# Token-mixing work of GpSimd on VectorE and ScalarE, S5 states reordered by ScalarE, modulation sums copied out by ScalarE

## The chip, the cores and the metric

One core of a Trainium2 chip runs the program. It has TensorE (PE in the profile, its weight loads PEld), VectorE (DVE), ScalarE (ACT), GpSimd (POOL) and SyncE (SP), which issues most of the transfers. The metric is the device time of one execution in microseconds, the median of several runs.

## The reference

Two layers work on 512 latent tokens and 256 context tokens of 1024 features, in float32. Of each layer:

```python
sh1, sc1, g1, sh2, sc2, g2 = ada_params(c, w_mod, b_mod)      # silu(c) @ w_mod + b_mod; the same for the context
mix = token_mixers(layer_norm(x) * (1 + sc1) + sh1, ...)
x = layer_norm(ALPHA * x + g1 * mix, ln1_g, ln1_b)
x = layer_norm(ALPHA * x + g2 * conv_ffn(layer_norm(x) * (1 + sc2) + sh2, ...), ln2_g, ln2_b)

def token_mixers(h):
    u, xl, g = split(h @ w_in)                # 512 columns each
    y  = s5_readout(s5_states of u, both directions) + d * u     # 32 groups of 16 channels, 64 complex states
    y  = gelu(y); y = y * sigmoid(y @ w_glu + b_glu)
    yl = (lru_forward + lru_backward)(conv4(xl)) * gelu(g)       # gated linear scans
    return concat(y, yl) @ w_out
```

`conv_ffn` is a gated up projection to 2 x 2816, a 3x3 depthwise convolution on the latent grid, gelu, and a down projection. The last layer gives latent tokens only.

## The kernel before, in words

Matrix products keep float32 accuracy by splitting each operand into a rounded high half and the low remainder, with three products per chunk (`mm3`, lines 165 to 172). `split` (158 to 163) makes the halves: the high one on ScalarE (or on the engine in `hi_eng`), the low one, a subtraction of 1024 columns for a weight, on the engine that is passed. `halves` (196 to 202) loads a weight and passes GpSimd for every weight of the program. `HIE = 'SG'` puts the high halves of the input projection's weights on ScalarE in layer 0 and on GpSimd (line 162) in layer 1.

A layer is one stretch of mixing, one of the output projection, one of the feed-forward part. Mixing goes over eight blocks `hb` of four S5 groups. `prep` builds a block's tables: two `outer` products (589 to 600, six operations of 512 columns each), in layer 0 one on GpSimd and one on VectorE, in layer 1 loaded from DRAM, then transposes and small products whose result goes through DRAM into `tm`. `enter` (693 to 712) makes the block's chunk inputs on PE, copies them out shifted by one chunk, in reverse order for the backward half of the partitions, and lets GpSimd spread the decay `r8` into `rt` (709). `leave` (714 to 744) turns the inputs by phase tables, scans them (727), turns them back, writes the states with six operations (735 to 738), the backward half in reverse order again, and PE makes the outputs from them. Between the blocks the list `FILL` puts projections (`u_part`, `x_part`, `g_part`) and LRU parts (`lru_part`, 771 to 814; line 813 sums the two directions on GpSimd). `glu` closes the S5 side, and lines 1023 and 1024 split the LRU side.

The phase tables (`s5_params`, 565 to 578) are products of coarse and fine phases; line 575 to 577 run once on GpSimd for the cosine half and once on VectorE for the sine half. Layer 1's are made during layer 0's feed-forward part.

`mods` (288 to 329) multiplies the condition with `w_mod` in 16 steps. Parts q = 1 and 2 run as filler beside the mixing. At the end VectorE adds a bias row of 256 KB to the PSUM sums (315), the gate is stored to DRAM (318), PE transposes the rest (323) and VectorE takes two of every 32 columns into `modc` (328).

The residual sum (826), the power of the normalization (352, 366) and the low halves of all other weights are GpSimd's in every stage. The order of each engine's instructions is made by a list scheduler from priorities and its own time model.

Of the kernel before, what the change touches and what calls it, by code (L numbers as in the profile page):

```python
# [21 lines left out]
DEPTH = 2  # L22
# [18 lines left out]
HIE = 'SG'  # L41
# [11 lines left out]
def body(ctx: ExitStack, tc: tile.TileContext, a, out):  # L53
# [87 lines left out]
    def small(shape):  # L141
        count[0] += 1
        n = int(np.prod(shape[1:]))
        return cp.tile(list(shape), F32, name=f"{where[0]}_st_{count[0]}", tag=f"st{n}", bufs={12: 4, 4: 8, 1: 6}[n])
# [11 lines left out]
    hi_eng = [None]  # L156
# [39 lines left out]
    def halves(src, hi, lo):  # L196

        raw = raws(hi.shape)
        with behind(hold[0]):
            weight_load[0] = load(raw, src)  # L200
        split(raw, hi, lo, G)
        return hi, lo
# [77 lines left out]
    def row_of(l, q, row_ring, load=load):  # L280
        where[0] = f"mod{l}{q}"
        row = row_ring([128, 2, 256])
        load(row, a["b_mod"][l, q])
        return row
# [3 lines left out]
    def mods(l, q, raw_ring, row_ring, bank, depth=2, bias_load=load, after=None):  # L288
# [3 lines left out]
        row = None if row_ring is raw_ring else row_of(l, q, row_ring, bias_load)  # L292
# [20 lines left out]
        if row is None:  # L313
            row = row_of(l, q, row_ring)
        V.tensor_add(row, ps, row)
        if q > 0:
            for t in range(4):
                load(gd[l][q - 1, :, 256 * t:256 * t + 256], row[32 * t:32 * t + 2, q - 1, :])
        tp = bank().rearrange("p (i r) -> p i r", i=4)
        hs = {0: (0, 1), 1: (1,), 2: (0,)}[q]  # L320
        for h in hs:
            for j in range(2):
                PE.transpose(tp[:, 2 * h + j, :], row[:, h, 128 * j:128 * j + 128], ident)
        for h in hs:
            base = {0: 8 * h, 1: 16, 2: 24}[q]
            add = 1.0 if q == 2 or (q == 0 and h == 1) else 0.0
            for j in range(2):
                V.tensor_scalar(modc[l][:, base + j:base + 8:2, :],
                                tp[:, 2 * h + j, :].rearrange("p (t w) -> p t w", w=32)[:, :, 0:2], add, None, op0=ADD)
# [112 lines left out]
    def s5_params(l, scratch, raw_slots, phase_slots, cs_slots, tmp_slot, load=load):  # L442
# [122 lines left out]
        for hb in range(8):  # L565
            yield
            step()
            gs = slice(4 * hb, 4 * hb + 4)
            cs = new(cs_slots[hb % 2], [128, 2, 4, 96])
            tt = new(tmp_slot, [128, 2, 4, 96])  # L570
            bh = lambda i: hi[:, i, gs].unsqueeze(3).to_broadcast([128, 4, 12, 8])
            bl = lambda i: lo[:, i, gs].unsqueeze(2).to_broadcast([128, 4, 12, 8])
            w = lambda x: x.rearrange("p g (a b) -> p g a b", b=8)
            for i, e, op in ((0, G, SUB), (1, V, ADD)):
                e.tensor_tensor(w(cs[:, i]), bh(0), bl(i), op=MUL)
                e.tensor_tensor(w(tt[:, i]), bh(1), bl(1 - i), op=MUL)
                e.tensor_tensor(cs[:, i], cs[:, i], tt[:, i], op=op)
            nc.sync.dma_start(csd[l, hb], cs.rearrange("p i g n -> p (i g n)"))
# [41 lines left out]
    class S5:  # L620
# [29 lines left out]
        def prep(self, hb):  # L650
# [6 lines left out]
            if l == 0:  # L657
                outer(fo, hb, 2, prm["cc"], False, G, self.tg)
                outer(ein, hb, 0, prm["bb"], True, V, self.tv)
            else:  # L660
                load(ein.rearrange("p i g j c -> p (i g j c)"), tabd[hb, 0])
                load(fo.rearrange("p i g j c -> p (i g j c)"), tabd[hb, 1])
# [30 lines left out]
        def enter(self, hb, et):  # L693
# [15 lines left out]
            G.tensor_scalar(rt, self.prm["r8"][:, gs].unsqueeze(2).to_broadcast([128, 4, 96]), 1.0, None, op0=MUL)  # L709
# [4 lines left out]
        def leave(self, hb, fo2, tm):  # L714
# [32 lines left out]
    class LRU:  # L747
# [23 lines left out]
        def __call__(self, m, xc, bank):  # L771
# [41 lines left out]
            G.tensor_tensor(hs[0][:, 0:keep], hs[0][:, 0:keep], hs[1][:, 0:keep], op=ADD)  # L813
# [38 lines left out]
    start = mods(0, 0, ring("m0", "m1", "v0", "v1", "a0", "a1", "a3", "r0", "r1"), ring("gs"), banks("p4"), 9, S.dma_start)  # L852
# [17 lines left out]
    for l in range(DEPTH):  # L870
# [4 lines left out]
        cols, coef = par[l]  # L875
        if l > 0:
# [8 lines left out]
        filler = itertools.chain(*(mods(l, q, md_r, md_r, md_b, after=first_w) for q in (1, 2)))  # L885
# [137 lines left out]
        for m in range(4):  # L1023
            split(ge[0][:, m, 0:ntok], ylru[m][0][:, 0:ntok], ylru[m][1][:, 0:ntok], G)
# [3 lines left out]
        where[0] = f"out{l}"  # L1028
        gt = new("v", [128, 2, D])
# [161 lines left out]
        nxt = iter(()) if last else mods(l + 1, 0, md_r, md_r, md_b)  # L1191

        def next_layer():

            par.append(columns(l + 1))
            yield
# [57 lines left out]
def lay_out(x):  # L1254
# [5 lines left out]
    y["b_mod"] = np.repeat(cut(x["b_mod"], 3, 2, 4, 256).transpose(0, 1, 3, 2, 4), 32, axis=2)  # L1260
# [41 lines left out]
```

## Time and profile before

| | us |
|---|---|
| median of 3 runs | 1757.7 (1757.34 to 1763.57) |
| the profiled execution | 1757.56 |
| its span | 1755.8 |
| busy in it: PE / DVE / ACT / POOL | 1562.5 / 1302.9 / 648.1 / 807.7 |
| layer 0: mixing | about 60 to 305 |
| layer 0: glu, output, feed-forward | 305 to about 1000 |
| from layer to layer | 1000 to 1060 |
| layer 1: mixing and glu | 1060 to 1300 |
| layer 1: output and feed-forward | 1300 to the end |

Busy is the time in which an engine has at least one instruction between its start and its end; an instruction that stands waiting for a resource after its start counts as busy. Idle time of an engine that is not the bottleneck costs nothing.

### The profile page before, as it was taken

What the parts mean: (1) busy time and instruction counts of PE and PEld (TensorE: products, weight loads), DVE (VectorE), ACT (ScalarE), POOL (GpSimd) and SP (SyncE); (2) the same over time, 40 slices, a digit from 0 to 9 for tenths busy, and PEclk for the clock granted to TensorE, in tenths of its full rate; (3) what the DMA queues carried; (4) which work ended last, traced back from release to release, by engine and by line L of the source; (5) the groups of instructions that cost most, each with busy time, mean ns of one, the idle gap of its engine ahead of it and who ended that gap; (6) DMA issues with size and microseconds to landing.
All of it is one profiled execution on the core that took longest, in us unless ns stands there. A gap on an engine that the chain in (4) does not pass through costs nothing. (4 is left out here: it accounts for less than half of the span.)

```text
span 1755.8 us, 22958 instructions
## 1 busy us (share of the span) xinstructions
PE 1562.5 (89%) x8824; PEld 1267.1 (72%) x8824; DVE 1302.9 (74%) x2104; ACT 648.1 (37%) x941; POOL 807.7 (46%) x496
## 2 busy tenths in 40 slices
PE   4768778898999999999999779989869899999996
PEld 1656655677888787887888658767547888888884
DVE  7999999478566995677689883889557476555587
ACT  2426445633633222222222136344661643323320
POOL 2567543548332244522325383533156454444474
PEclk8788898999899999999999898998879899999998
DMA  8335435742221212423334315665463333232231
GB/s 332 105 114 162 136 113 185 231 154 92 78 72 61 96 49 97 156 109 131 118 118 150 111 52 185 212 213 171 152 209 125 102 120 108 84 108 96 85 120 60
DMA packets 95359, 227.10 MB, mean 129 GB/s; under 512 B 28912, under 2 KB 39696, under 8 KB 95248
## 3 DMA queue, kind: packets, MB, share of 16 engines
q1 hardware_dynamic: 85456, 212.92, 36.3%
q10 hardware_dynamic: 9792, 12.71, 2.0%
q8 instruction: 69, 1.13, 0.3%
q14 instruction: 42, 0.34, 0.1%
HBM read 194.50 MB, written 31.10 MB: 128 GB/s over the span
## 5 line engine op out<-in xcount | busy, mean ns | idle before, releaser
L170 PE MATMUL banks<-ar,ar 128*128 128x512 f32 (+2 forms) x2152 | 777.6, 367 | 49.1 <-ACT ar L160 16.8
L171 PE MATMUL banks<-ar,ar 128*128 128x512 f32 (+2 forms) x2152 | 778.3, 363 | 17.3 <-DVE ar L396 7.8
L172 PE MATMUL banks<-ar,ar 128*128 128x512 f32 (+2 forms) x2152 | 770.9, 362 | 2.3 <-DVE ar L163 2.2
L163 POOL TENSOR_TENSOR ar<-ar,ar 128x1024 fp32r<-128x1024 f32 (+1 forms) x184 | 456.0, 2485 | 572.2 <-ACT ar L160 479.5
L170 PEld LDWEIGHTS banks<-ar,ar 128*128 128x128 f32 x2152 | 412.8, 193 | 134.0 <-ACT ar L160 20.8
L171 PEld LDWEIGHTS banks<-ar,ar 128*128 128x128 f32 x2152 | 415.7, 193 | 82.9 <-DVE ar L396 9.7
L172 PEld LDWEIGHTS banks<-ar,ar 128*128 128x128 f32 x2152 | 415.5, 193 | 65.7 <-DVE ar L163 4.2
L160 ACT ACTIVATE ar<-ar 128x1024 fp32r<-128x1024 f32 (+3 forms) x236 | 226.1, 976 | 496.7 <-PE banks L171 202.1
L1141 DVE SCALAR_TENSOR_TENSOR ar<-banks,cols,ar 128x441 f32<-128x441 f32 (+2 forms) x352 | 243.1, 691 | 41.8 <-ACT ar L1136 35.0
L1175 DVE TENSOR_TENSOR ar<-banks,ar 128x512 f32<-128x512 f32 x160 | 109.0, 685 | 117.4 <-PE banks L172 115.4
L163 DVE TENSOR_TENSOR ar<-ar,ar 128x512 fp32r<-128x512 f32 (+1 forms) x64 | 77.8, 1228 | 56.0 <-ACT ar L160 39.1
L826 POOL TENSOR_TENSOR ar<-ar 128x512 f32<-128x512 f32 x40 | 62.2, 1560 | 47.8 <-DVE ar L822 47.1
L1148 ACT ACTIVATE ar<-ar,cols 128x768 f32<-128x768 f32 (+1 forms) x44 | 36.6, 831 | 122.2 <-DVE ar L1141 71.4
L185 PE MATMUL banks<-ar,cond 128*32 128x256 f32 x192 | 64.8, 441 | 18.9 <-DMA ar<-in_w_mod_dram 18.9
L384 PE MATMUL banks<-ident,ar 128*128 128x128 f32 x176 | 36.5, 345 | 34.4 <-ACT ar L358 16.4
L188 PE MATMUL banks<-ar,cond 128*32 128x256 f32 x576 | 65.8, 441 | 0.0
L396 DVE TENSOR_TENSOR ar<-ar,ar 128x256 fp32r<-128x256 f32 (+1 forms) x64 | 41.4, 666 | 32.9 <-ACT ar L395 32.6
L783 PE MATMUL banks<-ar,ar 128*128 128x512 f32 (+1 forms) x128 | 54.7, 550 | 7.8 <-issue 6.9
L162 POOL TENSOR_SCALAR ar<-ar 128x1024 fp32r<-128x1024 f32 x12 | 35.5, 2958 | 49.2 <-PE banks L171 27.5
L384 PEld LDWEIGHTS banks<-ident,ar 128*128 128x128 f32 x176 | 26.2, 175 | 41.5 <-ACT ar L358 17.4
L1136 ACT ACTIVATE ar<-banks,cols 128x512 f32<-128x512 f32 x44 | 29.9, 679 | 69.7 <-PE banks L172 69.6
L185 PEld LDWEIGHTS banks<-ar,cond 128*32 128x32 f32 x192 | 15.8, 115 | 54.8 <-DMA ar<-in_w_mod_dram 32.4
(255 smaller groups left out, 1921.0 us busy)
## 6 DMA issues: line engine op xcount, KB each, us to landing
ar<-in_w_mod_dram SPq DMA_DIRECT2D x96, 512.0 KB
ar<-in_ffn_w_up_dram SPq DMA_DIRECT2D x88, 512.0 KB
ar<-in_ffn_w_down_dram SPq DMA_DIRECT2D x44, 512.0 KB
ar<-in_w_in_dram SPq DMA_DIRECT2D x24, 512.0 KB
tabd<-ar SPq DMA_DIRECT2D x16, 512.0 KB
ar<-tabd SPq DMA_DIRECT2D x16, 512.0 KB
csd<-ar SPq DMA_DIRECT2D x16, 384.0 KB
ar<-csd SPq DMA_DIRECT2D x16, 384.0 KB
```

The source lines that it names most:

```text
L160: S.activation(hi, src, AF.Copy)
L163: return lo_eng.tensor_tensor(lo, src, hi.bitcast(F32), op=SUB)
L170: PE.matmul(ps, wh, xh, start=first and k == 0, stop=False)
L171: PE.matmul(ps, wh, xl, start=False, stop=False)
L172: PE.matmul(ps, wl, xh, start=False, stop=last and k == nk - 1)
L185: ins = PE.matmul(*args, **kw)
L188: ins = PE.matmul(*args, **kw)
L384: PE.transpose(tp[:, o:o + 128], z[:, 128 * k:128 * k + 128], ident)
L783: PE.matmul(gp, w[:, d, i, :], xc[:, o:o + n], start=True, stop=True)
L826: G.tensor_tensor(xs_t[:, cs], xs_t[:, cs], tmp, op=ADD)
L1141: inst[0] = V.scalar_tensor_tensor(av[:, yo, xo], uv[:, yi, xi], tap(1 + dy, 1 + dx, ch), av[:, yo, xo], op0=MUL, op1=ADD)
L1175: V.tensor_tensor(acc, ps, acc, op=ADD)
```

## The change

- High halves of layer 1's input weights go from GpSimd to ScalarE (`HIE`), low halves of all weights loaded in the mixing (input projection and glu) from GpSimd to VectorE (`lo_eng`); from the output projection on they stay on GpSimd.
- GpSimd's `outer` product, its half of the phase tables, the sum of the LRU directions and the LRU side's low halves go to VectorE, the spread of `r8` to ScalarE.
- `leave` combines the turned states with two operations of full partitions on VectorE, and ScalarE copies them into `st` in three pieces (two in layer 1), reversed for the backward half.
- `mods`: ScalarE copies the sums out of PSUM, PE transposes them, ScalarE copies the used columns out, and VectorE adds the bias there, from a small table `modb`. A bias row is loaded for gates only, 128 KB, after the sums are there. The transposes use named places of PSUM.
- One of the four buffers for normalization statistics goes.

```diff
-HIE = 'SG'
+HIE = 'SS'
@@ halves
-        split(raw, hi, lo, G)
+        split(raw, hi, lo, lo_eng[0])
@@ mods, before the loop and after it
-        row = None if row_ring is raw_ring else row_of(l, q, row_ring, bias_load)
+        row = None if row_ring is raw_ring else row_ring([128, 2, 256])
...
-        V.tensor_add(row, ps, row)
-        if q > 0:
-            for t in range(4):
-                load(gd[l][q - 1, :, 256 * t:256 * t + 256], row[32 * t:32 * t + 2, q - 1, :])
+        S.activation(row, ps, AF.Copy)
...
-                PE.transpose(tp[:, 2 * h + j, :], row[:, h, 128 * j:128 * j + 128], ident)
+                PE.transpose(ends[h][:, j, :], row[:, h, 128 * j:128 * j + 128], ident)
+        for h in hs:
+            S.activation(row[:, h, 0:16].rearrange("p (j t v) -> p j t v", j=2, t=4),
+                         ends[h].rearrange("p j (t w) -> p j t w", w=32)[:, :, :, 0:2], AF.Copy)
...
-                V.tensor_scalar(modc[l][:, base + j:base + 8:2, :],
-                                tp[:, 2 * h + j, :].rearrange("p (t w) -> p t w", w=32)[:, :, 0:2], add, None, op0=ADD)
+                b = modb[:, base + j:base + 8:2].unsqueeze(2).to_broadcast([128, 4, 2])
+                V.scalar_tensor_tensor(modc[l][:, base + j:base + 8:2, :],
+                                       row[:, h, 8 * j:8 * j + 8].rearrange("p (t v) -> p t v", t=4), add, b, op0=ADD, op1=ADD)
+        if q > 0:
+            gate = row[:, q - 1, :]
+            bias = row_ring([128, 256])
+            load(bias, a["b_mod"][l, q - 1])
+            V.tensor_add(gate, gate, bias)
+            for t in range(4):
+                load(gd[l][q - 1, :, 256 * t:256 * t + 256], gate[32 * t:32 * t + 2, :])
@@ s5_params, prep, enter
-            for i, e, op in ((0, G, SUB), (1, V, ADD)):
+            for i, e, op in ((0, V, SUB), (1, V, ADD)):
...
-                outer(fo, hb, 2, prm["cc"], False, G, self.tg)
+                outer(fo, hb, 2, prm["cc"], False, V, self.tg)
...
-            G.tensor_scalar(rt, self.prm["r8"][:, gs].unsqueeze(2).to_broadcast([128, 4, 96]), 1.0, None, op0=MUL)
+            S.activation(rt, self.prm["r8"][:, gs].unsqueeze(2).to_broadcast([128, 4, 96]), AF.Copy)
@@ leave
+            for i, op in ((0, SUB), (1, ADD)):
+                V.tensor_tensor(t[:, i, :, k], t[:, i, :, k], u[:, i, :, k], op=op)
             st = v
-            for i, op in ((0, SUB), (1, ADD)):
-                V.tensor_tensor(st[0:64, i, :, k], t[0:64, i, :, k], u[0:64, i, :, k], op=op)
-                if n0 == 0:
-                    V.tensor_tensor(st[64:128, i, :, 31::-1], t[64:128, i, :, 0:32], u[64:128, i, :, 0:32], op=op)
-                V.tensor_tensor(st[64:128, i, :, 95:31:-1], t[64:128, i, :, 32:96], u[64:128, i, :, 32:96], op=op)
+            S.activation(st[64:128, :, :, 95:31:-1], t[64:128, :, :, 32:96], AF.Copy)
+            S.activation(st[0:64, :, :, k], t[0:64, :, :, k], AF.Copy)
+            if n0 == 0:
+                S.activation(st[64:128, :, :, 31::-1], t[64:128, :, :, 0:32], AF.Copy)
@@ LRU, the LRU side's split, the output projection
-            G.tensor_tensor(hs[0][:, 0:keep], hs[0][:, 0:keep], hs[1][:, 0:keep], op=ADD)
+            V.tensor_tensor(hs[0][:, 0:keep], hs[0][:, 0:keep], hs[1][:, 0:keep], op=ADD)
...
-            split(ge[0][:, m, 0:ntok], ylru[m][0][:, 0:ntok], ylru[m][1][:, 0:ntok], G)
+            split(ge[0][:, m, 0:ntok], ylru[m][0][:, 0:ntok], ylru[m][1][:, 0:ntok], V)
...
+        lo_eng[0] = G
```

## Rows read from the trace of the kernel before

**Rows 1.** The page: busy time (share, instructions), and slices in tenths, of PE and DVE.

```profile
PE 1562.5 (89%) x8824; PEld 1267.1 (72%) x8824; DVE 1302.9 (74%) x2104; ACT 648.1 (37%) x941; POOL 807.7 (46%) x496
...
PE   4768778898999999999999779989869899999996
...
DVE  7999999478566995677689883889557476555587
```

**Rows 2.** Stretches: length, busy of PE, PEld, DVE, ACT, POOL, granted clock, DMA, GB/s.

```profile
60.00:305.00 245.00, 192.53 (x1351) 151.21 (x1352) 241.07 (x370) 110.52 (x179) 134.82 (x97) 0.87 0.44 140
1000.00:1060.00 60.00, 42.88 (x179) 32.64 (x179) 45.96 (x80) 21.98 (x38) 43.74 (x40) 0.84 0.26 91
1060.00:1300.00 240.00, 208.29 (x1498) 163.13 (x1498) 166.06 (x213) 125.41 (x203) 92.19 (x59) 0.86 0.59 188
```

**Rows 3.** Timeline of DVE and POOL: start us, duration us, engine, line, operation, shapes.

```profile
206.24 1.65 POOL L596 TENSOR_TENSOR ar<-tab,cc 128x512 f32<-128x512 f32 x1
206.89 1.54 DVE L597 TENSOR_TENSOR ar<-ar,ar 128x512 f32<-128x512 f32 x1
...
209.23 0.54 DVE L735 TENSOR_TENSOR ar<-ar 64x384 f32<-64x384 f32 x1
209.79 0.29 DVE L737 TENSOR_TENSOR ar<-ar 64x128 f32<-64x128 f32 x1
...
212.28 0.68 DVE L599 TENSOR_TENSOR ar<-tab,bb 128x512 f32<-128x512 f32 x1
212.88 0.95 DVE L798 TENSOR_TENSOR ar<-ar,ar 128x768 f32<-128x768 f32 x1
...
1013.09 1.27 DVE L830 SCALAR_TENSOR_TENSOR ar<-ar,ln_st 128x1024 f32<-128x1024 f32 x1
```

**Rows 4.** Groups of DVE, 60 to 305 us: count, busy us, mean ns, idle before.

```profile
L735 DVE TENSOR_TENSOR ar<-ar 64x384 f32<-64x384 f32 x16 | 13.9, 867 | 0.3
L723 DVE TENSOR_TENSOR ar<-ar 128x768 f32<-128x768 f32 x8 | 11.9, 1483 | 0.0
...
L576 DVE TENSOR_TENSOR ar<-ar,ar 128x384 f32<-128x384 f32 x8 | 8.9, 1114 | 0.0
...
L738 DVE TENSOR_TENSOR ar<-ar 64x256 f32<-64x256 f32 x16 | 6.7, 418 | 0.0
```

**Rows 5.** Groups of POOL in the same stretch.

```profile
L163 POOL TENSOR_TENSOR ar<-ar,ar 128x1024 fp32r<-128x1024 f32 x10 | 27.1, 2708 | 26.1 <-ACT ar L160 26.1
L709 POOL TENSOR_SCALAR ar<-r 128x384 f32<-128x384 f32 x7 | 14.1, 2021 | 23.0 <-DVE ar L727 23.0
L600 POOL TENSOR_TENSOR ar<-ar,ar 128x512 f32<-128x512 f32 x7 | 13.3, 1907 | 0.2
...
L577 POOL TENSOR_TENSOR ar<-ar,ar 128x384 f32<-128x384 f32 x8 | 10.5, 1307 | 0.4
...
L813 POOL TENSOR_TENSOR ar<-ar,ar 128x768 f32<-128x768 f32 x3 | 5.4, 1815 | 15.0 <-DVE ar L810 15.0
```

**Rows 6.** Groups of ACT, 55 to 370 us, copies from SBUF to SBUF.

```profile
L160 ACT ACTIVATE ar<-ar 128x768 fp32r<-128x768 f32 x8 | 6.4, 832 | 4.2 <-DVE ar L935 4.2
...
L395 ACT ACTIVATE ar<-ar 128x256 fp32r<-128x256 f32 x4 | 1.7, 414 | 0.0
```

**Rows 7.** Timeline of POOL between the layers.

```profile
1040.84 2.78 POOL L162 TENSOR_SCALAR ar<-ar 128x1024 fp32r<-128x1024 f32 x1
...
1046.06 2.77 POOL L162 TENSOR_SCALAR ar<-ar 128x1024 fp32r<-128x1024 f32 x1
...
1051.16 1.25 POOL L826 TENSOR_TENSOR ar<-ar 128x512 f32<-128x512 f32 x1
```

**Rows 8.** Timeline of ACT, first and last of one LRU part's run.

```profile
1231.28 1.95 ACT L794 ACTIVATE ar<-ar,lru_st,coef 128x768 f32<-128x768 f32 x2
...
1238.04 1.76 ACT L803 ACTIVATE ar<-ar,lru_st 128x768 f32<-128x768 f32 x2
```

**Rows 9.** Waits of PE, 60 to 305 us: total us, times, longest us.

```profile
PE banks L742 <- DVE ar L738: 14.1, 3, 7.2
```

More of the change, by code (lines that the diff above doesn't have):

```diff
@@ L143, in small @@
         n = int(np.prod(shape[1:]))
-        return cp.tile(list(shape), F32, name=f"{where[0]}_st_{count[0]}", tag=f"st{n}", bufs={12: 4, 4: 8, 1: 6}[n])
+        return cp.tile(list(shape), F32, name=f"{where[0]}_st_{count[0]}", tag=f"st{n}", bufs={12: 3, 4: 8, 1: 6}[n])
     load = nc.sync.dma_start
@@ L153, in body @@
     V.memset(mhalf, -0.5)
-    hi_eng = [None]
+    hi_eng, lo_eng = [None], [V]
     def split(src, hi, lo, lo_eng):
@@ L278, in body, with ends_in, mods @@
     gd = [dram(f"gd{l}", [2, 2, D]) for l in range(DEPTH)]
[L280 to L284, printed above, removed]
+    def ends_in(b):
+        return [psum(b, [128, 4, 128])[:, 2 * h:2 * h + 2] for h in range(2)]
     tail, mod_load = [None], [None]
-    def mods(l, q, raw_ring, row_ring, bank, depth=2, bias_load=load, after=None):
+    modb = const("modb", [128, 32])
+    S.dma_start(modb, a["modb"][0])
+    def mods(l, q, raw_ring, row_ring, bank, ends, depth=2, after=None):
         ps = bank().rearrange("p (h j) -> p h j", h=2)
-        row = None if row_ring is raw_ring else row_of(l, q, row_ring, bias_load)
+        row = None if row_ring is raw_ring else row_ring([128, 2, 256])
         raws, ahead = [], iter([(h, kc) for h in range(2) for kc in range(KC)])
@@ L313, in mods @@
         if row is None:
-            row = row_of(l, q, row_ring)
-        V.tensor_add(row, ps, row)
-        if q > 0:
-            for t in range(4):
-                load(gd[l][q - 1, :, 256 * t:256 * t + 256], row[32 * t:32 * t + 2, q - 1, :])
-        tp = bank().rearrange("p (i r) -> p i r", i=4)
+            row = row_ring([128, 2, 256])
+        S.activation(row, ps, AF.Copy)
         hs = {0: (0, 1), 1: (1,), 2: (0,)}[q]
@@ L851, in body @@
         load(zt[t], token_rows(t))
-    start = mods(0, 0, ring("m0", "m1", "v0", "v1", "a0", "a1", "a3", "r0", "r1"), ring("gs"), banks("p4"), 9, S.dma_start)
+    start = mods(0, 0, ring("m0", "m1", "v0", "v1", "a0", "a1", "a3", "r0", "r1"), ring("gs"), banks("p4"), ends_in("p5"), 9)
     next(start)
@@ L875, in body @@
         cols, coef = par[l]
+        lo_eng[0] = V
         if l > 0:
@@ L884, in body @@
         first_w = [None]
-        filler = itertools.chain(*(mods(l, q, md_r, md_r, md_b, after=first_w) for q in (1, 2)))
+        filler = itertools.chain(*(mods(l, q, md_r, md_r, md_b, ends_in("p4"), after=first_w) for q in (1, 2)))
         def proj(col, tag, do_ctx=True, parts=False):
@@ L1190, in body @@
         md_b = banks(pvt[:, 1])
-        nxt = iter(()) if last else mods(l + 1, 0, md_r, md_r, md_b)
+        nxt = iter(()) if last else mods(l + 1, 0, md_r, md_r, md_b, [pvt[:, 1, 256 * h:256 * h + 256].rearrange("p (j x) -> p j x", j=2) for h in range(2)])
         def next_layer():
             par.append(columns(l + 1))
+            load(modb, a["modb"][l + 1])
             yield
@@ L1259, in lay_out @@
     y["cond"] = np.stack([x["c"].reshape(KC, 128), x["c_ctx"].reshape(KC, 128)]).transpose(2, 1, 0)
-    y["b_mod"] = np.repeat(cut(x["b_mod"], 3, 2, 4, 256).transpose(0, 1, 3, 2, 4), 32, axis=2)
+    b = x["b_mod"].reshape(DEPTH, 6, 4, 256)
+    y["b_mod"] = np.repeat(b[:, [2, 5]], 32, axis=2)
+    y["modb"] = cut(x["b_mod"], 6, 8, 128)[:, [0, 1, 3, 4]].reshape(DEPTH, 32, 128).transpose(0, 2, 1)
     y["w_in"] = cut(x["w_in"], KC, 128, 12, 128).transpose(0, 3, 2, 1, 4).copy()
```

## The prediction

> **What bounds the kernel now.** I read the page first: engine totals, then the forty slices. TensorE (PE) is busy 89% of the span and VectorE (DVE) 74%, but the slices show two kinds of stage [rows 1]. In slices 10 to 23, and again near the end, PE stands at 9: the feed-forward parts, which the change hardly touches. In slices 1 to 6 DVE stands at 9 and PE at 6 to 8: the token mixing of layer 0. The table of stretches puts numbers on it [rows 2]: from 60 to 305 us DVE is busy 241.07 of 245 us while PE has 192.53 at a mean granted clock of 0.87, and GpSimd (POOL) is busy 134.82 beside them. So DVE's end sets the time of layer 0's mixing; PE waits there mostly for DVE, above all for the last state operation, L738, 14.1 us in three waits [rows 9].
>
> Then I asked what those 241 us consist of. In the timeline a 128x512 multiply with two SBUF operands takes 0.68 us on DVE while POOL stands still (at 212.28), and an operation of the same size takes 1.54 us (at 206.89) where POOL has just started a read of its own (at 206.24, 1.65 us) [rows 3]. The groups by shape repeat it: L723 averages 1.48 us for 768 columns where one alone takes 0.95; L576 averages 1.11 and L735 0.87 for 384 columns where one alone takes 0.54 [rows 3, 4]. For these three groups the excess is 8 x 0.53 + 8 x 0.57 + 16 x 0.33 = 14 us; the same subtraction over all groups of that view, each against undisturbed runs of its own shape, gives about 74 us. So of DVE's 241 us in the stretch, about 167 are its own work and 74 are time spent beside POOL.
>
> **The profiled execution.** Its span is 1755.8 us, with 1.8 us around it 1757.6; the median of the three runs is 1757.7, so the sum below is made against 1757.6 and stands for the median too.
>
> **The change, part by part, layer 0 from 60 to 305 us.** POOL loses everything in this stretch but memsets of 0.1 us. DVE receives:
> - the output half of the S5 tables (`outer`): six lines like L600, 40 operations of 512 columns in the stretch (the other eight stand before 60 us), at 0.68 us = 27.2;
> - the low halves of the weights: 10 of 1024 columns. No such DVE operation is in the trace; the nearest is L830, two SBUF operands of 1024 columns, 1.27 us [rows 3, 5] = 12.7 (at 0.95, the price of 768 columns, 9.5; at POOL's 2.71, 27);
> - the first half of the phase tables: 24 of 384 columns like L577 at 0.54 = 13.0;
> - three sums of the two LRU scans (L813) at 0.95 = 2.9 [rows 3, 5].
> Together 55.8. DVE gives up the reordering: per block two each of L735, L737 and L738 (0.54, 0.29 and 0.42 undisturbed) become two of 384 columns at 0.54, so 2.50 - 1.08 = 1.42 us less, eight times 11.4 [rows 3, 4]. Net +44.4; consecutive DVE operations overlap a little in the trace (the durations add up to 25 us more than the busy time, over 370 operations), which takes 3 us off: +41. Excess beside POOL: -74. DVE's busy time goes from 241 to about **208 us**. If DVE stayed as full as now, the stretch would shrink by 33 us; if the freed time all went into new gaps, by nothing.
>
> I take **-22**, since a new gap is likely. Each block now ends with three ScalarE copies, of 768, 512 and 256 columns of 64 partitions: 0.83 + about 0.62 + 0.41 = 1.9 us [rows 6] (512 lies between those two rows), eight times 15 us of chain in which DVE must find other work. Before, it always had some queued; with a quarter of its queue gone, I let 11 us show. PE can follow: its 192.5 us of busy time fit in 223, and ScalarE is busy 110.5 of 245 [rows 2], so 8 x 1.9 of copies and 8 x about 0.5 for the r8 spread (L709, 2.0 us each on POOL [rows 5]) bring it to 130.
>
> The Trainium skill has a rule for this (SBUF — State Buffer, Who interferes with whom): VectorE with two SBUF inputs and a GpSimd operation that reads SBUF exclude each other through one shared read port, for the whole instruction. The rows agree in kind. In size the measured excess, 74 us beside 135 us of POOL, is about half of what full blocking by every POOL operation would make; by the rule taken literally POOL's spans hold waits as well, and no row separates them.
>
> **Before 60 us.** Eight table operations and three weight halves move onto DVE (8 x 0.68 + 3 x 1.27 = 9 us), which still waits for ScalarE in between. The first modulation is copied out by ScalarE instead of summed by DVE, with two more small ScalarE copies on the chain; the 256 KB bias row leaves ScalarE's DMA queue, 16 KB come in. Between -2 and +4; taken as 0, the work fitting in gaps that DVE has there.
>
> **From layer 0's end to layer 1's start, 1000 to 1060 us.** POOL is busy 43.74 of 60 us here [rows 2], and it carries the residual sums and the normalization's powers in order. Two roundings of layer 1's weights stand right between them (2.78 and 2.77 us), with the low halves behind, and the next residual sum comes only at 1051.16 [rows 7]. All of that leaves POOL: 5.5 us of roundings and two low halves of about 2.7 [rows 5], 11 us, against 2 x 1.27 on DVE (45.96 of 60 busy) and about 2 us on ScalarE (21.98 of 60). The chain through the last normalization to the first S5 block shortens by 2 to 9; I take **-6**.
>
> **Layer 1's mixing, 1060 to 1300 us.** PE is busy 208.29 and DVE 166.06 of 240: no engine is full [rows 2], so the chain per block counts. ScalarE's copies (two of 512 columns, 1.25 us) against 4 x 0.42 - 2 x 0.42 = 0.84 saved on DVE add 0.4 us and a handover each, about +5 over eight blocks. What goes is POOL's slowing of DVE in the same chain, of the same kind as above but less (POOL is busy 92 of 240), and the 5.5 us that a weight's two halves need on POOL [rows 5, 7], now about 2.3 (1.27 on DVE, and some 1.05 on ScalarE by the step from 256 to 768 columns in [rows 6]). Between -8 and +8; I take **-2**.
>
> **The rest.** The modulation's bias for a gate is loaded late, on SyncE's queue behind the weight stream, into the second of two stream buffers, so the next part's first load waits for the gate's sum: 0 to +4 per layer, hidden as long as PE has projections to do; I take nothing. In the feed-forward parts only layer 1's phase tables move (24 more DVE operations, 13 us in stretches where PE stands at 9), taken at nothing. The queues of SyncE and ScalarE gain one 16 KB load per layer.
>
> Sum: -22 - 6 - 2 = -30; 1757.6 - 30 = 1727.6, **1728 us**.
>
> **Rivals.**
> - *The freed time turns into gaps.* DVE no longer waits for POOL but for ScalarE's copies and PE, and layer 0's stretch stays near 240. For it: tables and states have one or two buffers each, so little can be done ahead. Against: eight blocks share 245 us, 30 us each, and the chain of one block, some ten DVE operations of 0.5 to 1 us with ScalarE's copies around them, is an estimated half of that. Gain only between the layers: 1757.6 - 6 = 1752 (1745 to 1763).
> - *Slower: ScalarE's queue comes into every block.* ScalarE runs in order, and one LRU part holds it from 1231.28 to 1239.80 without a gap, 8.5 us of functions and table loads [rows 8]. If a block's state copies stand behind such a run, the block waits half of it on average, 4 us, and 16 blocks pay 16 x 4.4 = 70; where DVE stays the bound (layer 0) the wait is hidden, so half of it, 35, decides, from about 2 us of waiting per block on. 1757.6 - 22 + 35 = 1771 (1764 to 1785).
> - *Slower: the excess has another cause.* If it is not POOL that stretches DVE's operations, DVE gets +41 in a stretch where it is full, and 1757.6 + 41 - 6 = 1793. Against it: the undisturbed rows above stand a few us from the stretched ones, with the same tiles. The Trainium skill's advice (Perfetto Trace Analysis, Optimizing Scalar/DVE Operations) speaks for this side: a saturated DVE is to be relieved, by ScalarE or even GpSimd. The same section adds that offloading between DVE and GpSimd may not help because they share a port; which of the two holds is what the change tries.
> - *More than forecast.* DVE stays full in layer 0 (-33) and layer 1 gets the whole -8, the transition -9: 1757.6 - 50 = 1708.
>
> **How the numbers follow.** Forecast 0.58 (1715 to 1745), more than forecast 0.08, gaps 0.18, ScalarE's queue 0.11, another cause 0.05. The range of 8 in 10 reaches from 1706 into the ScalarE case: 1706 to 1767; it leaves out the other cause, about half of ScalarE's queue and half of the larger gain, with some of the forecast's own tails. A change of about 0.5%, 8.8 us, is what a measurement of this kernel can tell from none. Below 1749: the forecast, the larger gain and a third of the gaps, 0.72; within: the rest of the gaps and a little more, 0.13; above 1766: 0.15.
>
> **What would show it.** Right: in layer 0's mixing no POOL work but memsets, DVE's 512-column operations at 0.68 us throughout, its busy time near 208 us, and glu's start some 20 us earlier; POOL's stretch between the layers without roundings. Wrong: DVE's operations as long as before with POOL idle; DVE waiting for ScalarE's copies (L742 of PE too) for more than 15 us in layer 0; state copies that start several us after DVE's last sum.

## The result, and the profile after

The changed kernel takes 1739.54 us (median of 4 runs, 1734.99 to 1740.85) against 1758.68 us: a ratio of 0.988 (95% interval 0.9855 to 0.9908). It is 19 us faster; 30 were forecast (1728). The profiled execution has a span of 1739.1 us and took 1740.85.

The page of the changed kernel, busy times and slices, beside [rows 1]:

```profile
PE 1551.7 (89%) x8824; PEld 1262.1 (73%) x8824; DVE 1264.9 (73%) x2194; ACT 703.7 (40%) x1028; POOL 525.3 (30%) x328
...
PE   4987898299899999999999888999778999999996
...
DVE  7998897457565997877689883788367576555587
```

POOL lost 282 us, DVE 38, ACT gained 56. PE has a slice at 2 (304 to 348 us) where it had an 8 before. The stretches, beside [rows 2]:

```profile
60.00:305.00 245.00, 207.47 (x1497) 161.69 (x1495) 212.21 (x403) 144.53 (x225) 1.40 (x13) 0.89 0.50 159
1000.00:1060.00 60.00, 45.82 (x186) 35.12 (x187) 45.20 (x81) 29.30 (x50) 38.71 (x37) 0.79 0.34 116
1060.00:1300.00 240.00, 209.74 (x1587) 164.11 (x1585) 157.15 (x219) 152.05 (x241) 24.99 (x24) 0.91 0.60 194
```

In the first line DVE's busy time is 212.21 us (forecast 208) and POOL's 1.40. The groups of DVE in that stretch, beside [rows 4], show that the excess is gone: 512 columns take 0.69 us and 384 columns 0.56, where one alone took 0.68 and 0.54 [rows 3].

```profile
L163 DVE TENSOR_TENSOR ar<-ar,ar 128x1024 fp32r<-128x1024 f32 x11 | 13.4, 1221 | 1.5 <-ACT ar L160 1.5
L609 DVE TENSOR_TENSOR ar<-ar,ar 128x512 f32<-128x512 f32 x16 | 11.0, 689 | 0.0
...
L743 DVE TENSOR_TENSOR ar<-ar 128x384 f32<-128x384 f32 x14 | 7.2, 558 | 0.0
```

The same for ScalarE's new copies (forecast 0.83, 0.62, 0.41, and 0.5 for r8):

```profile
L747 ACT ACTIVATE ar<-ar 64x768 f32<-64x768 f32 x7 | 5.9, 845 | 0.1
L746 ACT ACTIVATE ar<-ar 64x512 f32<-64x512 f32 x7 | 4.4, 628 | 7.3 <-DVE ar L743 7.1
L718 ACT ACTIVATE ar<-r 128x384 f32<-128x384 f32 x7 | 3.6, 520 | 6.5 <-DVE ar L736 6.5
L749 ACT ACTIVATE ar<-ar 64x256 f32<-64x256 f32 x7 | 2.9, 414 | 0.1
```

So the prices were right. Where the time went is another matter. This table holds starts read from the timelines, in us from the start of one profiled execution of each kernel: the first S5 scan of a layer ("first scan"), the first scan of layer 0's last block ("last scan"), the first product of the output projection's residual ("output") and the first residual product at the feed-forward part's end ("FFN end"). Below, a layer's mixing is the time from its first scan to its output. The kernels below the second line are those of the experiments.

| | first scan L0 | last scan L0 | output L0 | FFN end L0 | first scan L1 | output L1 | span |
|---|---|---|---|---|---|---|---|
| before | 115.4 | 297.9 | 370.4 | 1008.7 | 1105.8 | 1319.9 | 1755.8 |
| changed | 122.0 | 304.6 | 371.4 | 1006.7 | 1098.4 | 1304.4 | 1739.1 |
| e7, layer 1's weights only | 114.3 | 296.7 | 369.7 | 1005.3 | 1094.9 | 1286.4 | 1723.7 |
| e4, all but layer 1's weights | 121.9 | 298.9 | 366.2 | 1002.6 | 1099.3 | 1318.1 | 1754.5 |
| e2, states only | 114.7 | 297.4 | 377.6 | 1016.2 | 1111.0 | 1328.6 | 1768.5 |
| e1, states back | 122.5 | 306.8 | 368.3 | 1003.8 | 1096.2 | 1303.0 | 1739.5 |
| e10, ScalarE's work back | 115.8 | 301.5 | 367.7 | 1003.3 | 1094.6 | 1299.9 | 1735.6 |
| e8, layer 0 on POOL again | 118.2 | 300.6 | 379.9 | 1016.6 | 1107.9 | 1306.8 | 1743.9 |
| e6, last LRU part later | 122.8 | 297.5 | 364.5 | 999.7 | 1091.3 | 1294.5 | 1731.5 |
| e9, half the tables left out | 113.1 | 263.2 | 329.7 | 967.0 | 1058.7 | 1265.8 | 1700.7 |

Layer 0's mixing, from which 22 of the 30 us were to come, gave nothing: its output starts at 371.4 instead of 370.4. The 16.7 us of the span are 3.0 in layer 0's output and feed-forward part (638.3 to 635.3), 5.3 between the layers (97.1 to 91.8 from its end to layer 1's first scan), 8.1 in layer 1's mixing (214.1 to 206.0) and 1.2 behind it, less the 1.0 of layer 0.

**Where layer 0's time stayed.** From 60 us to the last scan, the kernel before:

```profile
60.00:298.00 238.00, 185.83 (x1316) 147.91 (x1316) 234.23 (x359) 105.16 (x168) 134.82 (x97) 0.86 0.43 138
```

and the changed one:

```profile
60.00:304.60 244.60, 207.47 (x1497) 161.69 (x1495) 211.81 (x402) 144.13 (x225) 1.40 (x13) 0.89 0.50 159
```

DVE's work is 22 us less, but its idle time went from 3.8 to 32.8 us. The eight blocks keep their pace to the tenth: (297.9 - 115.4) / 7 = 26.1 us before, (304.6 - 122.0) / 7 = 26.1 after. What DVE waited for from 60 to 324 us (total us, times, longest), the first four of fifteen lines; the same view of before has two lines, 6.5 and 2.9 us:

```profile
DVE ar L815 <- ACT ar L814: 9.8, 4, 6.2
DVE ar L693 <- ACT ar L692: 4.4, 3, 2.5
DVE ar L732 <- DMA ar<-csd: 3.3, 2, 1.9
DVE ar L809 <- ACT lru_st L800: 2.7, 2, 1.5
```

Some 21 of the 32 us are waits for ScalarE, and the largest of them is not for the new copies but for the square roots of the LRU parts (L814). The longest case, DVE's timeline ahead of the last block:

```profile
283.33 0.69 DVE L609 TENSOR_TENSOR ar<-ar,ar 128x512 f32<-128x512 f32 x1
290.24 1.83 DVE L815 SCALAR_TENSOR_TENSOR ar<-ar,ar 128x768 f32<-128x768 f32 x2 [6.22 <-ACT ar L814]
...
300.00 0.17 DVE L693 TENSOR_TENSOR ar<-banks,dd 128x16 f32<-128x16 f32 x1
...
304.60 0.95 DVE L736 TENSOR_TENSOR_SCAN ar<-ar 128x384 f32<-128x384 f32 x1
```

DVE stands 6.22 us, then does the whole LRU part, and only then comes the last block's first operation (L693) and its scan (L736). ScalarE's timeline has the state copies of the block before in the same knot: DVE made the states at 282.39, and they are copied at 291.06, behind the LRU's roots.

```profile
287.97 1.28 ACT L814 ACT_TABLE_LOAD   x1
289.26 1.77 ACT L814 ACTIVATE ar<-ar,lru_st 128x768 f32<-128x768 f32 x2
291.06 0.63 ACT L746 ACTIVATE ar<-ar 64x512 f32<-64x512 f32 x1
```

What the freed time bought is filling work done early: the last reverse scan of an LRU part starts at 294.3 instead of 316.5 us, and PE, with its filling gone, idles behind 305 us, where the last block's chain is all that is left.

### The profile page after: what moved, and what is told of

The parts are those of the page before. It is cut to its first block, busy times and chain, and to the rows that moved or that the text cites. A ratio compares the mean times of both kernels' runs of the same rounds, so it can differ in the third digit from the quotient of the medians.

```text
span 1739.1 us, 22976 instructions
## 1 busy us (share of the span) xinstructions
PE 1551.7 (89%) x8824; PEld 1262.1 (73%) x8824; DVE 1264.9 (73%) x2194; ACT 703.7 (40%) x1028; POOL 525.3 (30%) x328
## 5 line engine op out<-in xcount | busy, mean ns | idle before, releaser
L163 POOL TENSOR_TENSOR ar<-ar,ar 128x1024 fp32r<-128x1024 f32 x148 | 366.2, 2482 | 669.5 <-ACT ar L160 602.4
L160 ACT ACTIVATE ar<-ar 128x1024 fp32r<-128x1024 f32 (+2 forms) x248 | 239.0, 982 | 482.5 <-PE banks L171 211.0
L163 DVE TENSOR_TENSOR ar<-ar,ar 128x512 fp32r<-128x512 f32 (+2 forms) x100 | 113.9, 1152 | 88.6 <-ACT ar L160 70.8
L405 DVE TENSOR_TENSOR ar<-ar,ar 128x256 fp32r<-128x256 f32 (+1 forms) x64 | 34.4, 555 | 34.3 <-ACT ar L404 34.2
L393 PEld LDWEIGHTS banks<-ident,ar 128*128 128x128 f32 x176 | 26.7, 178 | 37.7 <-ACT ar L367 16.7
```

Of the source, the lines that this page charges most:

```text
L160: S.activation(hi, src, AF.Copy)
L163: return lo_eng.tensor_tensor(lo, src, hi.bitcast(F32), op=SUB)
L393: PE.transpose(tp[:, o:o + 128], z[:, 128 * k:128 * k + 128], ident)
```

## The experiments

Medians, each with the ratio to the kernel before on the same chip and its 95% interval. The changed kernel's ratio is 0.988; by the widths of the intervals, another kernel can be told from it when its ratio differs by about 0.0035 (6 us) or more.

**e1_states_dve: the changed kernel, states by VectorE again.**

```diff
-            for i, op in ((0, SUB), (1, ADD)):
-                V.tensor_tensor(t[:, i, :, k], t[:, i, :, k], u[:, i, :, k], op=op)
...
-            S.activation(st[64:128, :, :, 95:31:-1], t[64:128, :, :, 32:96], AF.Copy)
...
+                V.tensor_tensor(st[0:64, i, :, k], t[0:64, i, :, k], u[0:64, i, :, k], op=op)
...
```

> The changed kernel (1739.5 us) with the states written by VectorE's six operations again, everything else as changed. Theory A (the gain of layer 0 went into ScalarE's queue: a block's three state copies stand behind LRU functions, up to 7.7 us): no state waits for ScalarE, layer 0's last S5 output comes at about 314 to 318 instead of 323.8 us, layer 1's blocks lose a handover each, total 1728 to 1735. Rival B (the handover is hidden, and VectorE's own queue sets the end of layer 0): VectorE gets back 8 x 1.4 us of work in layer 0, the last output comes at 323 to 328 and the total is 1739 to 1746. Rival C (the reordering of the queue by the scheduler outweighs either): outside both.

1740.35 us (0.991, 0.989 to 0.9927): B in the total, no measurable difference from the changed kernel, and neither theory in the place: the last output comes at 322.4 us, 1.4 us earlier. The copies are not what holds layer 0.

**e2_only_states: the kernel before, with the new `leave` alone.**

```diff
-                V.tensor_tensor(st[0:64, i, :, k], t[0:64, i, :, k], u[0:64, i, :, k], op=op)
...
+            S.activation(st[64:128, :, :, 95:31:-1], t[64:128, :, :, 32:96], AF.Copy)
...
```

> The kernel before (1757.7 us) with one part of the change alone: the states put in chunk order by ScalarE's copies. Theory A (copies queue behind LRU functions): layer 0's last S5 output comes 4 to 10 us later than before (309.6), layer 1's last one 4 us later or more, total 1763 to 1772. Rival B (the handover is hidden by VectorE's full queue, from which 11 us go): layer 0 0 to 8 us shorter, total 1749 to 1758.

1768.91 us (1.007, 1.0054 to 1.0089): A's total, in another way than A said. The last S5 output is only 1.1 us later (310.7), but the last LRU reverse scan of layer 0 starts at 327.3 instead of 316.5 us, and the output at 377.6 instead of 370.4. It is the LRU parts that end later, not the blocks. By itself this part of the change costs 12 us (0.5 to 0.9%); inside the change, by e1, nothing that can be measured. So its price can't be read off the copies; it depends on what else stands in ScalarE's queue and DVE's.

**e3_ylru_pool: the changed kernel, the LRU side's low halves on GpSimd again.**

```diff
-            split(ge[0][:, m, 0:ntok], ylru[m][0][:, 0:ntok], ylru[m][1][:, 0:ntok], V)
+            split(ge[0][:, m, 0:ntok], ylru[m][0][:, 0:ntok], ylru[m][1][:, 0:ntok], G)
```

> The changed kernel with the low halves of the LRU side (four operations of 128x768 or 128x512) on GpSimd again. Theory A (in layer 0 two of these stand on VectorE in front of the last block's turn, beside GpSimd's first low halves of the output weights, and push the last block's chain): the time from layer 0's last scan to its last S5 output falls from 19 to 12 to 14 us, total 1732 to 1735. Rival B (the last block is held by ScalarE's queue, 12.3 us of PE's wait for the last copy): stays at 17 to 20 us, total 1738 to 1742. Rival C (GpSimd's reads slow VectorE again): 1742 or more.

1743.62 us (0.9926, 0.9908 to 0.9945): C's total. The last output comes 20.6 us behind the last scan, so A's forecast failed, though the cause that it named is in the changed kernel's timeline:

```profile
306.97 5.45 POOL L163 TENSOR_TENSOR ar<-ar,ar 128x1024 fp32r<-128x1024 f32 x2 [26.44 <-ACT ar L160]
307.18 6.05 DVE L163 TENSOR_TENSOR ar<-ar,ar 128x768 fp32r<-128x768 f32 x2
313.16 0.95 DVE L740 TENSOR_TENSOR ar<-ar 128x768 f32<-128x768 f32 x1
```

Two low halves of 768 columns take 6.05 us beside POOL's two of 1024 (one alone, just ahead, takes 0.94), and the last block's turn (L740) stands behind them. Made by GpSimd instead (e3), they hold up the same chain from there, as C had it: GpSimd makes five low halves in a row, and DVE's two state operations of 384 columns beside them, which take 1.02 us for the block before last of the changed kernel, take 5.19 for the last block.

```profile
302.28 13.01 POOL L163 TENSOR_TENSOR ar<-ar,ar 128x768 fp32r<-128x768 f32 x5 [24.12 <-ACT ar L160]
...
310.52 5.19 DVE L743 TENSOR_TENSOR ar<-ar 128x384 f32<-128x384 f32 x2
```

**e4_w1_pool: the changed kernel, layer 1's weights on GpSimd again.**

```diff
-HIE = 'SS'
+HIE = 'SG'
...
-        lo_eng[0] = V
+        lo_eng[0] = V if l == 0 else G
```

> The changed kernel with the high and low halves of layer 1's mixing weights on GpSimd as before the change, all else as changed. Theory A (the gain between the layers and in layer 1, 5 and 9 us, is the roundings and low halves that left GpSimd's chain): first scan of layer 1 about 5 us later, total 1749 to 1755. Rival B (layer 1 gains from the tables, sums and spreads that no longer slow VectorE): total 1739 to 1744.

1759.4 us (1.0017, 1.0001 to 1.0033): the whole gain is gone. Between the layers it is 96.7 us again, as before (97.1), so that term is the weights'; and layer 1's mixing is 218.9 us, 4.8 longer than before the change. A is right on the cause, and its sum was too small.

**e7_only_w1: the kernel before, with that part alone.**

```diff
-HIE = 'SG'
+HIE = 'SS'
...
-        split(raw, hi, lo, G)
+        split(raw, hi, lo, lo_eng[0])
...
+        lo_eng[0] = V if l > 0 else G
```

(and G again from the output projection on)

> The kernel before (1757 us) with one part of the change alone: layer 1's mixing weights (high halves by ScalarE, low halves by VectorE instead of both by GpSimd). Theory A (this part carries the whole gain, since undoing it alone gave it all back): total 1737 to 1744, layer 1's mixing 10 to 16 us shorter from first scan to the output projection. Rival B (it is worth something only with the other work gone from GpSimd too): total 1750 to 1758.

1731.6 us (0.984, 0.9817 to 0.9862): better than A's range. One part of the change gives 28 us, the whole change 19. Its layer 0 is that of before (369.7), the way between the layers takes 89.6 us, layer 1's mixing 191.5 (its profiled execution, 1725.5, is the fastest of its runs, 6 us below their median). PE in layer 1, beside the last of [rows 2]: more work in the same 240 us, at a granted clock of 0.96 instead of 0.86.

```profile
1060.00:1300.00 240.00, 219.95 (x1639) 172.53 (x1638) 178.09 (x240) 134.70 (x208) 48.59 (x38) 0.96 0.63 203
```

Why so much: POOL's timeline of the kernel before, two weights in a row.

```profile
1205.66 2.80 POOL L162 TENSOR_SCALAR ar<-ar 128x1024 fp32r<-128x1024 f32 x1
...
1208.55 2.50 POOL L163 TENSOR_TENSOR ar<-ar,ar 128x1024 fp32r<-128x1024 f32 x1
1211.01 4.21 POOL L162 TENSOR_SCALAR ar<-ar 128x1024 fp32r<-128x1024 f32 x1
1216.94 1.27 POOL L813 TENSOR_TENSOR ar<-ar,ar 128x512 f32<-128x512 f32 x1 [1.72 <-DVE ar L810]
1218.16 2.35 POOL L163 TENSOR_TENSOR ar<-ar,ar 128x1024 fp32r<-128x1024 f32 x1
```

The first weight takes 5.4 us; the second 9.5 from 1211.01, since its low half stands on POOL behind an LRU sum that waits for DVE. The roundings as a group, 1060 to 1300 us, show what they wait for themselves:

```profile
L162 POOL TENSOR_SCALAR ar<-ar 128x1024 fp32r<-128x1024 f32 x9 | 27.2, 3018 | 32.8 <-PE banks L171 27.5 <-DMA ar<-in_w_in_dram 5.3
```

A rounding starts when PE has freed the buffer, and PE can use the weight when both halves are made, so the two stand between PE's release of a buffer and its next use. In e7 the same two weights begin on ScalarE, behind the same wait:

```profile
1188.09 1.06 ACT L160 ACTIVATE ar<-ar 128x1024 fp32r<-128x1024 f32 x1 [2.55 <-PE banks L171]
...
1194.02 1.06 ACT L160 ACTIVATE ar<-ar 128x1024 fp32r<-128x1024 f32 x1 [2.85 <-PE banks L171]
```

and their low halves end on DVE at 1192.78 and 1200.95. From the start of the high half to the end of the low one eleven of layer 1's twelve weights in the kernel before (1040.84 to 1220.51; the twelfth is made earlier) take 8.0 us on average (5.2 to 13.2), e7's eleven, paired in order, 4.7 (2.3 to 9.3). Eleven times 3.2 is 36 us. That this became the 28 us of the medians is argued and not shown: the view of PE's waits from 1060 to 1320 us of the kernel before has ten lines, 33 us in all, and none of them names GpSimd; nor does one of PE's weight loads.

The timelines show a part of the gain in another place. In all these kernels the output of layer 1 starts 34 to 38 us behind the last reverse scan of its last LRU part. ScalarE's functions of that part, from the small copy behind its gates (L789) to the last root (L803), take 15.9 us in the kernel before, since two gelus of the g parts, with table loads of their own, and high halves (L160) stand among them:

```profile
1265.30 0.19 ACT L789 ACTIVATE lru_st<-ar 128x1 f32<-128x1 f32 x1
1265.50 1.28 ACT L924 ACT_TABLE_LOAD   x1
...
1279.42 1.76 ACT L803 ACTIVATE ar<-ar,lru_st 128x768 f32<-128x768 f32 x2
```

In e7 these stand behind the run, and it takes 9.2 us:

```profile
1236.02 0.20 ACT L789 ACTIVATE lru_st<-ar 128x1 f32<-128x1 f32 x1
...
1243.47 1.77 ACT L803 ACTIVATE ar<-ar,lru_st 128x768 f32<-128x768 f32 x2
```

So of the 22.6 us by which e7's mixing is shorter (214.1 to 191.5), some 7 lie in the order of ScalarE's queue, which came with the edit.

**e8_l0_pool: the changed kernel, layer 0's work back on GpSimd.**

```diff
-                outer(fo, hb, 2, prm["cc"], False, V, self.tg)
+                outer(fo, hb, 2, prm["cc"], False, G, self.tg)
...
-        lo_eng[0] = V
+        lo_eng[0] = V if l > 0 else G
```

(and the phase tables' first half and layer 0's LRU sums)

> The changed kernel with GpSimd's layer 0 work given back (one table product, the first half of the phase tables, the low halves of layer 0's weights, layer 0's LRU sums), layer 1 as changed. Theory A (freeing VectorE from GpSimd in layer 0 is worth nothing, since the blocks' chain and not VectorE's occupation sets layer 0's end): output projection of layer 0 at 368 to 375 us, total 1737 to 1745. Rival B (the freed time did shorten layer 0, and the copies by ScalarE, 12 us in the kernel before by themselves, took it back): layer 0's end 8 to 15 us later, total 1748 to 1756, VectorE's excess beside GpSimd back.

1747.69 us (0.9934, 0.9917 to 0.995), just below B's total, with layer 0's output 8.5 us later, as B had it: 8 us slower than the changed kernel. DVE's long operations are back, 1167 ns where the changed kernel has 689:

```profile
L731 DVE TENSOR_TENSOR ar<-ar 128x768 f32<-128x768 f32 x8 | 11.2, 1405 | 0.0
L609 DVE TENSOR_TENSOR ar<-ar,ar 128x512 f32<-128x512 f32 x8 | 9.3, 1167 | 0.0
```

So freeing DVE in layer 0 is worth 8 us with ScalarE's new work in place. In the table e10 against e7 gives its worth without that work: 369.7 to 367.7, 2 us.

**e9_half_tables: the changed kernel without one table product for seven of layer 0's blocks.**

```diff
-                outer(fo, hb, 2, prm["cc"], False, V, self.tg)
+                if hb == 0:
+                    outer(fo, hb, 2, prm["cc"], False, V, self.tg)
```

> The changed kernel without the output half of the S5 tables for seven of layer 0's eight blocks (42 operations of 512 columns, 29 us of VectorE; the blocks use what stands in the buffers). Theory A (VectorE's own work still sets layer 0's pace): layer 0's end 15 to 29 us earlier, total 1711 to 1725. Rival B (handovers along the blocks' chain set it): layer 0's end 0 to 8 us earlier, total 1732 to 1740.

1702.63 us (0.9682, 0.9662 to 0.9703), beyond A: layer 0's output starts 41.7 us earlier for 42 operations of 0.69 us, 29 us. From 60 us to the last scan:

```profile
60.00:263.20 203.20, 173.81 (x1352) 137.00 (x1351) 176.59 (x351) 124.44 (x197) 1.41 (x13) 0.91 0.58 184
```

DVE's work is 35 us less (some filling now ends behind the last scan) and its idle time 26.6 us, nearly as much as in the changed kernel. So DVE's work does set the blocks' pace: without six operations of 0.69 us, 4.1 us a block, it falls from 26.1 to (263.2 - 113.1) / 7 = 21.4 us. The edit takes away DVE's work together with PE's waits for its results, so it doesn't tell the two apart; and it tells what leaving the product out is worth, not what its place on GpSimd was worth (e8).

**e6_l3_later: the changed kernel, layer 0's last LRU part two places later.**

```diff
-FILL = ('u1 x0 u2 u3|l0 x1||g0 l1 x2 g1|l2 x3|l3|g2|g3 s', ...
+FILL = ('u1 x0 u2 u3|l0 x1||g0 l1 x2 g1|l2 x3|g2|g3|l3 s', ...
```

> The changed kernel (1739.5 us) with layer 0's last LRU part put two places later among the fill between the blocks (behind the last g parts). Theory A (the last blocks wait in order behind that LRU part: VectorE stood idle 6.2 us for its functions at 284 us with the last block's input correction queued behind it, and the last block's copies 7.7 us): layer 0's last S5 output comes at 310 to 317 instead of 323.8 us and the output projection starts 3 to 10 us earlier than 371; total 1729 to 1737. Rival B (the LRU part then ends last and the output projection waits for it, as before the change): output projection at 370 or later, total 1738 to 1746.

1731.24 us (0.9842, 0.9822 to 0.9862): A, 8 us faster than the changed kernel. The last scan comes at 297.5, the last output at 310.3 instead of 323.8, the output projection 6.9 us earlier; DVE's idle time to the last scan falls from 32.8 to 23.5:

```profile
60.00:297.50 237.50, 205.23 (x1502) 159.53 (x1501) 214.00 (x398) 139.34 (x220) 14.73 (x17) 0.90 0.55 174
```

This shows a part of layer 0's gaps: the last blocks stood behind an LRU part in the queues of DVE and ScalarE.

**e11_old_mods, e12_no_state_r8, e10_no_act_work: ScalarE's new work taken back in parts.** e11 gives back the modulation, e12 the states and r8, e10 all three. Of e12:

```diff
-            S.activation(rt, self.prm["r8"][:, gs].unsqueeze(2).to_broadcast([128, 4, 96]), AF.Copy)
+            G.tensor_scalar(rt, self.prm["r8"][:, gs].unsqueeze(2).to_broadcast([128, 4, 96]), 1.0, None, op0=MUL)
...
-            S.activation(st[0:64, :, :, k], t[0:64, :, :, k], AF.Copy)
...
```

and of e11:

```diff
-        S.activation(row, ps, AF.Copy)
+        V.tensor_add(row, ps, row)
...
```

> The changed kernel (1739.5 us) with all work given back that the change had laid on ScalarE except the high halves: the states (VectorE again), the spread of r8 (GpSimd again) and the modulation's copies (VectorE's sum again). What is left of the change is the weights and GpSimd's tables, sums and low halves on VectorE. Theory A (ScalarE's extra functions, some 17 us of its time in layer 1, cost layer 1 the 14 us by which its mixing is longer than where the weights alone were moved, 206 against 191.5 us; freeing VectorE in layer 0 is worth 8): layer 1's mixing 190 to 197 us, total 1718 to 1728. Rival B (the loss is in the sums and low halves that VectorE got, or in the modulation's order): 1734 to 1745.

> The changed kernel with the modulation as before (VectorE adds a bias row that is loaded ahead, no ScalarE copies), all else as changed. Theory A (states and r8 spread are what ScalarE had too much of): 1736 to 1742. Rival B (the late load of the gate's bias and the new modulation chain hold the stream of modulation weights, and PE's waits for that stream, 22 us in layer 0, are the loss): 1724 to 1734.

> The changed kernel with the states on VectorE and the spread of r8 on GpSimd again, the modulation as changed. Theory A (with both gone from ScalarE the S5 blocks and the LRU parts of layer 1 no longer stand behind each other): 1722 to 1732, where giving back the states alone left 1740. Rival B (neither is the loss; it is the modulation): 1737 to 1743.

1737.85 us (0.9876, 0.9854 to 0.9899), 1742.75 (0.9905, 0.9882 to 0.9929) and 1738.15 (0.9885, 0.9863 to 0.9907): none differs from the changed kernel's 1739.5 by what can be told. Layer 1's mixing is 205.3, 208.1 and 207.1 us, not 191.5: the theory that ScalarE's extra functions make layer 1 longer fell in all three. What they do show: with the old modulation the first scan comes at 115.8 and 115.9 us, with the new one at 121.9 to 122.8 in the changed kernel, e1, e6 and e12. So the new modulation costs 6 us at the start of layer 0, though not by itself: with the new modulation and the tables back on GpSimd (e8) it comes at 118.2, and without most of one table product (e9) at 113.1. The 6 us are recovered before the layer's end (e12's output starts at 366.8, e11's at 366.3).

**e13_x3_before_l2: e6 with layer 1's last x part ahead of the third LRU part.**

```diff
-... 'x0 u1 u2 u3|l0 x1|g0 l1|x2 g1|l2 x3||l3|g3 g2 s')
+... 'x0 u1 u2 u3|l0 x1|g0 l1|x2 g1|x3 l2||l3|g3 g2 s')
```

> The kernel of e6_l3_later (1731 us) with one further edit of the order: in layer 1 the last x part is emitted ahead of the third LRU part. Theory A (what layer 1 loses against the weights alone is an order in VectorE's queue: the last convolution stands behind the third LRU part's combination, which waits up to 6.5 us for ScalarE's square root, and the last gates on TensorE, the last LRU part and glu's gelu follow it): the last convolution ends at 114 to 125 us after layer 1's first scan instead of 136, layer 1's mixing falls from 203 to 192 to 198 us, total 1719 to 1726. Rival B (the place of this convolution is a symptom, and the sums and low halves on VectorE or ScalarE's occupation set the end of layer 1): mixing 200 to 207, total 1728 to 1736.

What led to it: DVE's timeline of the changed kernel has the last convolution (L772) behind an LRU combination that waits 6.54 us for the roots,

```profile
1222.88 1.83 DVE L815 SCALAR_TENSOR_TENSOR ar<-ar,ar 128x768 f32<-128x768 f32 x2 [6.54 <-ACT ar L814]
...
1225.49 0.48 DVE L772 SCALAR_TENSOR_TENSOR ar<-banks,cols,ar 128x254 f32<-128x254 f32 x1
...
1234.14 0.76 DVE L772 SCALAR_TENSOR_TENSOR ar<-banks,cols,ar 128x511 f32<-128x511 f32 x1
```

and that of e7 has four of its six operations (L761 there) ahead of the same combination (L804):

```profile
1217.41 1.53 DVE L761 SCALAR_TENSOR_TENSOR ar<-banks,cols,ar 128x511 f32<-128x511 f32 x2
...
1225.14 0.96 DVE L804 SCALAR_TENSOR_TENSOR ar<-ar,ar 128x768 f32<-128x768 f32 x1 [1.08 <-ACT ar L803]
```

1730.82 us (0.9834, 0.9806 to 0.9861): B. The edit did what it should, the last convolution starts at 1209.23, 118 us behind the first scan instead of 136:

```profile
1209.23 0.75 DVE L772 SCALAR_TENSOR_TENSOR ar<-banks,cols,ar 128x511 f32<-128x511 f32 x1
```

but layer 1's mixing went only from 203.2 to 199.7 us, the last S5 output came 7 us later (1230.4), and the total stayed. In e7 the last of these operations starts at 1228.1, 133 us behind the first scan, so its place was not what sets e7 apart. Kernels that share layer 1's assignment of engines (the changed one, e6, e8, e9, e13) lie between 199 and 207 us there, so some of it is the order of the queues; why e7 has 191.5 is open in part. Some 6 us can be the choice of the execution, since e7's profiled one is that much below its median. Of the work in layer 1's mixing e10 differs from e7 only in the LRU sums and the LRU side's low halves, which are on DVE; e3 gave the low halves back in the changed kernel and has 204.2, and the sums were not tried alone. The trace names one more candidate, which wasn't tried alone. In the changed kernel ScalarE's last LRU run holds two functions of g parts with table loads of their own, and glu's gelu waits for the end of it:

```profile
1252.12 1.28 ACT L936 ACT_TABLE_LOAD   x1
1253.41 0.60 ACT L936 ACTIVATE ar<-banks 128x512 f32<-128x512 f32 x1
1254.03 1.28 ACT L806 ACT_TABLE_LOAD   x1
...
1266.68 2.56 ACT L977 ACTIVATE ar<-ar,glu_st 128x512 f32<-128x512 f32 x4
```

In e7 these functions come behind glu's gelu, which starts at 1246.56. They do so in e13 too: its run takes 9.4 us where that of e6 takes 15.0, which bears on the 3.5 us by which its mixing is shorter, but its total is that of e6.

## Why the forecast was right, and where it was wrong

The sign and the range held (1739.5 in 1706 to 1767); 11 of the 30 us were missing, and the sources were other ones. That the total fell inside the range is luck in part: the stage that was to give 22 us gave nothing, and layer 1's mixing, taken at 2, gave 8.

- **DVE's busy time in layer 0**: forecast 208, measured 212. The excess beside POOL went from 74 to about 4 us by the same subtraction, and e8 brings it back. DVE's low halves of 1024 columns took 1.22 us (1.27 taken). On the Trainium skill's rule (SBUF — State Buffer, Who interferes with whom: DVE's operations with two SBUF inputs and POOL's reads exclude each other) the trace agrees, now from both sides: in the rows shown at e3 two operations on either engine take 6.05 and 5.45 us in the same seven microseconds.
- **The gaps in layer 0**: this step failed. 11 us of new gaps were allowed for, 29 came (3.8 to 32.8). To the last scan that is 234.2 - 22.4 of work and 3.8 + 29.0 of gaps, 244.6 us in place of 238.0; the work is less down than in the stretch to 305 us (241 to 212) since more filling lies ahead of the last scan now. The prediction looked for them at the state copies; most are waits for ScalarE's LRU functions and small corrections. State copies several us behind DVE's last sum, which it named as a sign of being wrong, did occur (7.7 us at 291), but giving the copies back (e1) or all of ScalarE's new work (e10) does not shorten the blocks' pace (26.3 and 26.5 us a block). That DVE, at 98% busy before, had hidden such waits with other work fits all of this and was not tried by itself. One named wait, an LRU part ahead of the last blocks, is shown (e6, 8 us); the rest is told by the table of waits only.
- **Before 60 us**: taken as 0 within -2 and +4. The first scan came 6.6 us later, by the modulation together with the tables on DVE (e8, e10, e11), and the layer recovered it.
- **Between the layers**: -6 forecast, -5.3 measured, and it is the roundings and low halves that left POOL (e4: 96.7 us with them back, before 97.1).
- **Layer 1's mixing**: -2 forecast, -8.1 measured, just outside the bounds. The term was named, 5.5 us per weight against 2.3, and mis-sized: with its waits it was 8.0 against 4.7 us, for eleven weights, where the sum set it off against the copies by a guess. Alone this part takes 22.6 us off the mixing (e7, 214.1 to 191.5), an order of ScalarE's queue included; within the change 12.9 (e4 against the changed kernel, 218.9 to 206.0). What the rest of the change costs layer 1, 5 to 14 us, isn't the states (e1), the states and r8 (e12), the modulation (e11), all three together (e10) or the LRU side's low halves (e3); it stays open.
- **The rest**: 0 forecast, -3.0 and -1.2 measured, within what all these kernels differ by there (634.9 to 638.5 us from layer 0's output to its end).
- **The rivals**: the one in which the freed time turns into gaps is what layer 0 did (its 1752 took layer 1 as unchanged). ScalarE's queue at 1771 is nearly what the states cost in the kernel before (e2, 1768.9), but through the LRU parts, not through the blocks. That DVE's excess had another cause is refuted by the groups.
- **A reading**: of the slices counted as PE's full ones, 10 to 23, the last two stand at 7 (966 to 1054 us, on the way to layer 1); no term of the sum hangs on it.

e7, e6 and e13 lie at 1731 us, 8 below the changed kernel and 28 below the kernel before. e7 is the smallest of the edits.

## What to carry to other kernels

A busy share of 98% says that an engine always had something to do, not that everything it did was on the path: before crediting the time that leaves it, ask for each stage what it will wait for once its queue runs empty, and put that wait on the other side of the sum. Look at operations that prepare another engine's input, here the halves of eleven weights at some 3 us each, before those that merely fill an engine. When a change has several parts, try each of them alone: one gave 28 us, another cost 12, and all together gave 19.

## What was not expected of the hardware

- Two subtractions of 768 columns on DVE took 6.05 us beside two of 1024 on POOL (5.45), against 0.94 and 2.35 for one (the row just ahead, and the last row of POOL's at e7): three times as long for DVE, while the largest mean in [rows 4] is 1.48 us for 768 columns.
- PE's mean granted clock in 1060 to 1300 us went with the place of layer 1's weights: 0.86 to 0.88 in the three kernels that have them on GpSimd (before, e2, e4), 0.90 to 0.96 in the eleven others, 0.91 in the changed kernel, 0.96 in e7, where PE did 1639 matrix products against 1498. Which part of e7's gain is the clock, no run tells.
